# A closing projection: more chunks with seven block products, remainders added by DMA, squares a chunk later

## The chip, the cores and the metric

The kernel runs on one core of one Trainium2 chip. The metric is device time in microseconds (us), from the core's own execution, as a median over runs. The engines have short names in the profile: PE is TensorE (matrix products; PEld is the loading of its stationary operand), DVE is VectorE, ACT is ScalarE, POOL is GpSimd, and SP is SyncE, which here issues most of the loads. A trailing q (SPq, POOLq) means the engine's queue of DMA issues.

## The reference

The program is a two-layer trunk over 256 tokens of width 2048, in float32. The part that matters here is its end: the second layer's feed-forward block, its down projection, the residual and the final norm.

```python
def conv_ffn(xn, w_up, conv_w, conv_b, w_down):
    S = xn.shape[1]
    h = xn @ w_up
    hp = jnp.pad(h, ((0, 0), (CONV_W - 1, 0), (0, 0)))
    h = sum(hp[:, k:k + S] * conv_w[k] for k in range(CONV_W)) + conv_b
    gate, val = jnp.split(h, 2, axis=-1)
    return (jax.nn.silu(gate) * val) @ w_down
...
    h = h + conv_ffn(rmsnorm(h, f_norm[l]), f_w_up[l], f_conv_w[l], f_conv_b[l], f_w_down[l])
...
return rmsnorm(h, final_norm)
```

`w_down` is 5632 x 2048, the activations are 256 x 5632, the result 256 x 2048. Everything before this projection is the same in both kernels.

## The kernel before, in words

**Products in three parts.** Every large product is computed in a rounded 32-bit format (fp32r). Each operand is split into a rounded part (`whi`, ScalarE, line 110 or 88) and a remainder (`wlo`, VectorE: the value less the rounded part, line 111 or 89). A product of two split operands is then three matrix products: rounded x rounded, rounded x remainder, remainder x rounded.

**The stream.** `Stream` takes a list of items, one for each weight chunk of 512 KB (128 partitions x 1024 values). At step i of its `run` it issues, in this order, the load of item i + 6 on SP's queue (line 78), the split of item i + 3, the products of item i, and one step of each side task that is pending (`advance`). Engines work in order on what they are given and wait on semaphores. Raw chunks lie in four buffers used in turn (a ring), the split parts `whi` and `wlo` in four each. So a load waits until the raw chunk four chunks back has been split, and a split waits until the products of the item four back are done.

**The closing projection** has 88 chunks. Its output is worked on by token (128 tokens in each of two blocks, `tb`), 512 columns at a time for blocks 0 to 2 and 256 at a time for the last 512 columns (`short_block` and `last_block`). A plain chunk covers 256 rows of `w_down` and 512 columns: 24 products 256 columns wide.

**Seven products in place of eight.** A chunk can be seen as a 2 x 2 grid of blocks on both sides: two blocks of rows, two halves of the columns, two blocks of tokens. Eight block products can be had from seven, if sums of blocks are formed first (a scheme of Strassen's kind). Such a chunk takes two items: `seven` forms the weight sums (`weight_sums`, lines 490 to 493) and splits three of the raw blocks (line 88 and 89, 768 wide) for the first item, and splits the four sums (1024 wide) for the second. The first item has 9 products 256 columns wide, the second 12, together 21. The sums of the activations are formed once, in pairs of chunks, by `sums_of_blocks` into `X1`, which is free by then. What several chunks add to common partial results is collected in a second PSUM tile `m` and folded into the residual stream `h` by `sums_into_residual` (lines 564 to 580). Before, 1 chunk of block 0 and 8 each of blocks 1 and 2 go this way.

**Behind each block,** the side task `final(blk)` adds the block to `h` (line 435), squares it for the norm with a sum along the row (line 436, ScalarE), and multiplies by the final norm's gains (line 449). `output` (lines 625 to 648) ends the program: the last columns' sum of squares, the root, the scaling, the stores. In `last_block` the products of the first 128 tokens are finished first, and those of the last four chunks for the other 128 are held back, so that the first output overlaps them (`HELD` = 4).

The order of chunks is made by `order_of`, which spreads the seven-product chunks evenly among the plain ones.

Of the kernel before, what the change touches and what calls it, by code (L numbers as in the profile page):

```python
# [17 lines left out]
P = 128  # L18
D = 2048
# [15 lines left out]
SUMMED = (4, 5, 8, 9, 12, 13, 16, 17)  # L35
# [9 lines left out]
class Stream:  # L45
# [38 lines left out]
    def two_parts(self, src, at):  # L84

        n = src.shape[1]
        hi, lo = self.room(at)
        self.nc.scalar.activation(hi[:, :n], src, AF.Copy)
        self.nc.vector.tensor_tensor(lo[:, :n], src, hi[:, :n].bitcast(F32), op=OP.subtract)  # L89
        return hi, lo  # L90
# [70 lines left out]
def order_of(blk):  # L161


    some = SUMMED[:1] if blk == 0 else SUMMED
    plain, seven = [c for c in range(KF // 2) if c not in some], list(some)
    head = 19 if blk == 0 else 2
    out = [(c, False) for c in plain[:head]]
    plain = plain[head:]
    n, m = len(plain), len(seven)
    for i, c in enumerate(plain):  # L170
        while len(seven) * n > (n - i - 1) * m and seven:
            out.append((seven.pop(0), True))
        out.append((c, False))
    return out


def build(ctx, tc, d, out):
# [259 lines left out]

    def final(blk):
        def done(ps):
            while state["summed"] < min(blk + 1, 3):  # L440
                yield
            ss = ph.keep("ss", [P, 2, 5])
            n = ps.shape[2]
            cols = slice(blk * 512, blk * 512 + n)
            for tb in range(2):
                add_block(tb, cols, ps[:, tb, :], ss[:, tb, blk:blk + 1])
                yield
                hh = by_token()[:, tb, cols]
                nc.vector.tensor_tensor(hh, hh, ph.keep("gains", [P, D])[:, cols], op=OP.mult)
                yield  # L450
            if blk == 3:
                v, nv = ph.keep("v", [P, 2]), ph.keep("nv", [P, 2])
                nc.vector.tensor_reduce(v, ss[:, :, :4], axis=AX.X, op=OP.add)
                nc.vector.tensor_scalar(v, v, 1.0 / D, EPS, op0=OP.mult, op1=OP.add)
                nc.vector.tensor_scalar(nv, v, -0.5, None, op0=OP.mult)
# [3 lines left out]
    def block_sums():  # L459

        return X1.rearrange("p (q r) w -> p q (r w)", r=2).rearrange("p q (f l t) -> p q f l t", f=4, l=2)

    def sums_of_blocks(q, pair):

        H = ffn_h()
        x, f = (room().rearrange("p (q i t) -> p q i t", q=2, i=4) for _ in range(2))
        hi, lo = (block_sums()[:, q:q + 2, :, i, :] for i in range(2))
# [747 lines left out]
```

## Time and profile before

| | |
|---|---|
| median of 3 runs | 2180.82 us (2178.99 to 2181.57) |
| profiled execution | 2178.91 us, its span from first to last instruction 2177.0 us |
| granted TensorE clock | 0.999 |
| TensorE busy | 2165.4 us, 99% of the span, 18689 products |
| VectorE busy | 1535.1 us, 71% |
| ScalarE busy | 1163.4 us, 53% |
| GpSimd busy | 27.4 us, 1% |
| bytes moved by DMA | 447.32 MB, 205 GB/s on average |

A row of a group reads: line, engine, operation, output and inputs by the program's names, shapes, count, then the busy time of the group and the mean time of one in ns, then the time for which the engine stood idle before such an instruction and what ended it. A row of a timeline gives start and duration in us, and in brackets the idle time ahead of it. A row of stretches gives the window, then for each engine its busy time and its count of instructions, then the granted clock, the share of the DMA engines and GB/s. A row of a wait gives who waited for whom, the total in us, how many times and the longest. A row of DMA issues ends with the median time from issue to landing. TensorE's instructions overlap in its pipeline, so the durations listed for single products exceed the distance between them.

### The profile page before, as it was taken

To read this page: it belongs to the slowest core of one execution; us is meant where nothing else is said; L and a number is where in the kernel's file an instruction comes from. 1 tells how busy PE (TensorE), PEld (TensorE's weight loads), DVE (VectorE), ACT (ScalarE), POOL (GpSimd) and SP (SyncE) were. 2 spreads that over 40 slices of the span, in tenths; PEclk is the share of its full clock that TensorE was granted. 3 is DMA by queue.
4 is the path that set the end of the run, shared out by engine and by line. 5 is a ranking of instruction groups with operands and counts; after the bars stand their busy time and mean duration, and the time that the engine had idled before them with its cause. 6 is when DMAs were issued, how large, how long until landed. Compare 5 with 4: busy or idle time off the path is not lost.

```text
span 2177.0 us, 45111 instructions
## 1 busy us (share of the span) xinstructions
PE 2165.4 (99%) x18689; PEld 2148.9 (99%) x18689; DVE 1535.1 (71%) x2188; ACT 1163.4 (53%) x1560; POOL 27.4 (1%) x46
## 2 busy tenths in 40 slices
PE   9999999999999999999999999999999999999998
PEld 9999999999999999999999999999999999999998
DVE  6696687777777745556787676678777777778874
ACT  6665555555555544444554665546555555554553
POOL 0000000000000000000001200000000000000000
PEclk9999999999999999999999999999999999999999
DMA  8686565565666566666778776567756565655574
GB/s 312 191 245 200 192 198 194 187 201 188 200 192 195 195 193 195 194 194 184 246 238 263 235 220 199 184 223 220 246 194 194 194 194 187 201 191 177 196 215 153
DMA packets 153230, 447.32 MB, mean 205 GB/s; under 512 B 25584, under 2 KB 44800, under 8 KB 152640
## 3 DMA queue, kind: packets, MB, share of 16 engines
q1 hardware_dynamic: 151488, 440.48, 63.1%
q0 software_dynamic: 1072, 3.41, 0.6%
q8 instruction: 146, 2.39, 0.5%
q10 hardware_dynamic: 464, 0.55, 0.1%
q14 instruction: 60, 0.49, 0.1%
HBM read 430.72 MB, written 13.65 MB: 204 GB/s over the span
## 4 chain that ended last, share of the span: by engine, by line
PE 99%; DVE 1%; DMA 0%; ACT 0%; SPq 0%; issue 0%; DVEq 0%; ACTq 0%
PE ps L212 97%; PE mp L1072 0%; DMA mlp_vt<-a_in_v 0%; DVE wlo L111 0%; ACT whi L110 0%; PE ps L1067 0%; PE ps L1066 0%; PE ps L1065 0%; PE mp L1071 0%; DVE wlo L89 0%; DVE h L435 0%; SPq L78 0%; ACT sq L436 0%; SPq L652 0%; DVE h L647 0%
## 5 line engine op out<-in xcount | busy, mean ns | idle before, releaser
L111 DVE TENSOR_TENSOR wlo<-raw,whi 128x1024 fp32r<-128x1024 f32 x761 | 923.7, 1219 | 390.6 <-ACT whi L110 386.9
L110 ACT ACTIVATE whi<-raw 128x1024 fp32r<-128x1024 f32 x761 | 800.8, 1058 | 674.3 <-PE ps L212 599.2
L212 PE MATMUL ps<-X,whi 128*128 128x256 f32 (+1 forms) x6476 | 824.0, 279 | 0.0
L212 PEld LDWEIGHTS ps<-X,whi 128*128 128x128 f32 x6476 | 776.2, 188 | 6.5
L212 PE MATMUL ps<-X,wlo 128*128 128x256 f32 x3328 | 445.3, 276 | 0.0
L212 PEld LDWEIGHTS ps<-X,wlo 128*128 128x128 f32 x3328 | 409.9, 188 | 1.6
L212 PE MATMUL ps<-whi,ffn_H 128*128 128x256 f32 (+1 forms) x1232 | 201.5, 277 | 0.5 <-ACT whi L110 0.4
L212 PE MATMUL ps<-whi,X 128*128 128x256 f32 (+1 forms) x1136 | 183.1, 279 | 0.4 <-ACT whi L110 0.4
L212 PEld LDWEIGHTS ps<-whi,ffn_H 128*128 128x128 f32 x1232 | 172.9, 188 | 1.3 <-ACT whi L110 0.9
L212 PE MATMUL ps<-ffn_H,whi 128*128 128x256 f32 x1408 | 173.9, 276 | 0.0
L822 DVE SCALAR_TENSOR_TENSOR ffn_room<-ffn_room,col 128x255 f32<-128x255 f32 x352 | 161.8, 481 | 6.4
L212 PEld LDWEIGHTS ps<-ffn_H,whi 128*128 128x128 f32 x1408 | 166.1, 188 | 0.0
L212 PE MATMUL ps<-whi,att_X 128*128 128x256 f32 (+2 forms) x970 | 164.3, 285 | 0.0
L212 PEld LDWEIGHTS ps<-whi,X 128*128 128x128 f32 x1136 | 155.0, 188 | 2.0 <-ACT whi L110 0.6
L212 PE MATMUL ps<-wlo,ffn_H 128*128 128x256 f32 (+1 forms) x615 | 139.2, 277 | 1.5 <-DVE wlo L111 1.5
L212 PEld LDWEIGHTS ps<-whi,att_X 128*128 128x128 f32 x970 | 135.3, 188 | 3.5
L388 DVE TENSOR_TENSOR ffn_room<-ps,rB 128x512 f32<-128x512 f32 x76 | 52.6, 692 | 116.1 <-PE ps L212 116.1
L818 ACT ACTIVATE ffn_room<-ffn_room,col 128x256 f32<-128x256 f32 x176 | 96.3, 595 | 50.0 <-DVE ffn_room L388 50.0
L212 PE MATMUL ps<-wlo,X 128*128 128x256 f32 (+1 forms) x566 | 116.7, 279 | 0.0
L212 PE MATMUL ps<-wlo,att_X 128*128 128x256 f32 (+2 forms) x476 | 105.4, 286 | 0.0
L212 PEld LDWEIGHTS ps<-wlo,ffn_H 128*128 128x128 f32 x615 | 101.1, 188 | 2.0 <-DVE wlo L111 1.9
L212 PE MATMUL ps<-ffn_H,wlo 128*128 128x256 f32 x704 | 94.1, 276 | 0.0
(196 smaller groups left out, 1518.0 us busy)
## 6 DMA issues: line engine op xcount, KB each, us to landing
raw<-up SPq DMA_DIRECT2D x352, 512.0 KB, 4.1
raw<-down SPq DMA_DIRECT2D x154, 512.0 KB, 4.2
raw<-a_in_u SPq DMA_DIRECT2D x32, 512.0 KB, 4.2
raw<-a_out SPq DMA_DIRECT2D x32, 512.0 KB, 3.9
raw<-b_q SPq DMA_DIRECT2D x32, 512.0 KB, 4.5
raw<-kvf_v SPq DMA_DIRECT2D x32, 512.0 KB, 4.9
raw<-b_g SPq DMA_DIRECT2D x32, 512.0 KB, 4.4
raw<-b_out SPq DMA_DIRECT2D x32, 512.0 KB, 4.0
```

What stands on the lines that cost most here:

```text
L110: self.nc.scalar.activation(h, raw, AF.Copy)
L111: self.nc.vector.tensor_tensor(l, raw, h.bitcast(F32), op=OP.subtract)
L212: nc.tensor.matmul(o, a, b, start=start, stop=stop, skip_group_check=True)
L388: nc.vector.tensor_tensor(a, src, rB[:, None, :].to_broadcast([P, 2, T]), op=OP.mult)
L818: nc.scalar.activation(c[:, m, :], a[:, m, :], AF.Identity, scale=w[2], bias=column(C_CONVB + l * 2 * KF + f))
L822: nc.vector.scalar_tensor_tensor(c[:, m, n:], a[:, m, :T - n], w[k], c[:, m, n:], op0=OP.mult, op1=OP.add)
```

## The change

The projection becomes four blocks of 512 columns, all through `seven_block`. Which chunk is of which kind is written out by hand in `ORDERS`: P is plain, S has seven products, D is plain with an added remainder. Block 0 has 22 P; blocks 1 and 2 have P P and five times S D S P; block 3 has ten S, five D and seven P. So S goes from 17 to 30. The chunks with sums are now always the first ten, and the sums of their activations take less room: one of four sums is written over a block of the activations `H` that no later product reads as it was.

In a D chunk VectorE has nothing to do. `added_parts` lets ScalarE write the negated rounded value into `lo`, lets a DMA on GpSimd's queue add the raw chunk to it, with source and destination in SBUF, and lets ScalarE write the rounded value into `hi`. The products with `lo` are put last in such a chunk (`late`): 16 products with `hi`, then 8 with `lo`.

`final` puts a step between the addition and the square, so that the square is issued a chunk after the addition; the last step of `sums_into_residual` comes one chunk earlier. In block 3 the last four plain chunks are held back for the second token block, as `last_block` did; the two column halves of that block are finished one after the other, `closing` squares the first half while the second's products run, and `output` ends as before. The load of ScalarE's table for the square root moves from block 3's end to block 2's.

```diff
-SUMMED = (4, 5, 8, 9, 12, 13, 16, 17)
+PLAIN, SEVEN, ADDED = range(3)
+SUMMED = tuple(range(10))
+ORDERS = ("P" * 22, "PP" + "SDSP" * 5, "PP" + "SDSP" * 5, "PSDSPSDSSDSPSDSSDSPPPP")
...
+    def added_parts(self, src, at):
+
+        hi, lo = self.room(at)
+        self.nc.scalar.activation(lo, src, AF.Copy, scale=-1.0)
+        self.nc.gpsimd.dma_start(lo, src, accum_op=OP.add)
+        self.nc.scalar.activation(hi, src, AF.Copy)
         return hi, lo
...
+    kinds = ["PSD".index(k) for k in ORDERS[blk]]
+    seven = list(SUMMED[:kinds.count(SEVEN)])
+    others = [c for c in range(KF // 2) if c not in seven]
+    return [((seven if k == SEVEN else others).pop(0), k) for k in kinds]
...
     def final(blk):
         def done(ps):
-            while state["summed"] < min(blk + 1, 3):
-                yield
...
+            while state["summed"] < blk:
+                yield
+            ss, gains, _, _ = kept()
+            cols = slice(blk * 512, (blk + 1) * 512)
             for tb in range(2):
-                add_block(tb, cols, ps[:, tb, :], ss[:, tb, blk:blk + 1])
-                yield
                 hh = by_token()[:, tb, cols]
-                nc.vector.tensor_tensor(hh, hh, ph.keep("gains", [P, D])[:, cols], op=OP.mult)
-                yield
...
+                nc.vector.tensor_tensor(hh, hh, ps[:, tb, :], op=OP.add)
+                yield
+                nc.scalar.activation(sq, hh, AF.Square, accum_out=ss[:, tb, blk:blk + 1])
+                yield
+                nc.vector.tensor_tensor(hh, hh, gains[:, cols], op=OP.mult)
+            if blk == 2:
                 nc.scalar.activation(warm, ones, AF.Sqrt)
...
+    def closing(tb, half, ps):
+
+        ss, gains, v, nv = kept()
+        v, nv, r = (a[:, tb:tb + 1] for a in (v, nv, rcol))
+        o = by_token()[:, tb, :]
+        assert state["summed"] == 3
+        if not half:
+            cols = slice(1536, 1536 + T)
+            add_block(tb, cols, ps, ss[:, tb, 3:4])
+            nc.vector.tensor_tensor(o[:, cols], o[:, cols], gains[:, cols], op=OP.mult)
+            nc.vector.tensor_reduce(v, ss[:, tb, :4], axis=AX.X, op=OP.add)
+            nc.vector.tensor_scalar(v, v, 1.0 / D, EPS, op0=OP.mult, op1=OP.add)
+            nc.vector.tensor_scalar(nv, v, -0.5, None, op0=OP.mult)
+        else:
+            output(tb, ps)
...
+        own = sums_kept()[:, q:q + 2]
+        for hi, lo, src in ((own[:, :, :, 0, :], own[:, :, :, 1, :], f[:, :, 1:, :]),
+                            (other[:, :, 0, 1, :], other[:, :, 1, 1, :], f[:, :, 0, :])):
+            nc.scalar.activation(hi, src, AF.Copy)
+            nc.vector.tensor_tensor(lo, src, hi.bitcast(F32), op=OP.subtract)
...
+        def tiles(c, i, hi, lo, tbs, halves, wide=0, late=False):
+            todo = [(j, tb, o) for j in range(2) for tb in tbs for o in ((0, hi), (0, lo), (1, hi))]
+            if late:
+                todo.sort(key=lambda o: o[2][1] is lo)
...
+                if close and i > last - HELD:
+                    held.append((c, i, hi, lo))
+                    tiles(c, i, hi, lo, (0,), (0, 1))
+                else:
+                    tiles(c, i, hi, lo, (0, 1), (0, 1), 0 if close else wide_next(), kind == ADDED)
...
             nc.vector.tensor_tensor(hh[:, :, :T], hh[:, :, :T], m[:, 1:, :T].to_broadcast([P, 2, T]), op=OP.add)
-            yield
             nc.vector.tensor_tensor(hh[:, :, :T], hh[:, :, :T], one[:, 1:, :], op=OP.subtract)
...
-    for blk in range(3):
-        seven_block(blk, d["down1"][22 * blk:22 * blk + 22], order_of(blk), final(blk), sums_into_residual(blk))
-    short_block(d["down1s"][:11], ffn_h, KF, final(3))
-    last_block(d["down1s"][11:], ffn_h, KF)
+    for blk in range(4):
+        seven_block(blk, d["down1"][22 * blk:22 * blk + 22], final(blk), sums_into_residual(blk),
+                    closing if blk == 3 else None)
...
-    arrays["down1"], arrays["down1s"] = tok_chunks(down1[:, :1536]), feat_chunks(down1[:, 1536:])
+    arrays["down1"] = tok_chunks(down1)
```

More of the change, by code (lines that the diff above doesn't have):

```diff
@@ L556, in seven @@
             s.chunk(None, mult_sums, TOK_AT, split=lambda _: s.two_parts(held["t"], TOK_AT))
-        for i, (c, s7) in enumerate(order):
-            if s7:
-                seven(c, i, not any(f for _, f in order[:i]))
+        for i, (c, kind) in enumerate(order):
+            if kind == SEVEN:
+                seven(c, i)
             else:
-                plain(c, i)
+                plain(c, i, kind)
     def sums_into_residual(blk):
```

143 lines of the change are left out of this document (63 added, 80 removed).

## The prediction

> **What bounds the kernel now.** I read the page first, its busy times and its chain of waits.
>
> ```profile
> PE 2165.4 (99%) x18689; PEld 2148.9 (99%) x18689; DVE 1535.1 (71%) x2188; ACT 1163.4 (53%) x1560; POOL 27.4 (1%) x46
> PE 99%; DVE 1%; DMA 0%; ACT 0%; SPq 0%; issue 0%; DVEq 0%; ACTq 0%
> ```
>
> TensorE is busy for 99% of the span and is 99% of the chain. A change gains only by giving it fewer products or by taking away an instant in which it waits. The chain in order of time gives the price of a product, the stretches of the closing projection what is lost there now.
>
> ```profile
> 2139.98 29.37 PE ps L212 x259
> ...
> 2169.37 0.43 DVE h L435
> ...
> 1934.00:1990.00 56.00, 56.00 (x492) 55.87 (x491) 47.07 (x56) 27.91 (x30) 0.00 (x0) 1.00 0.62 201
> 1990.00:2052.00 62.00, 61.12 (x537) 60.73 (x537) 52.65 (x69) 32.35 (x37) 0.00 (x0) 1.00 0.62 202
> 2052.00:2112.00 60.00, 58.85 (x517) 58.45 (x516) 49.89 (x62) 31.19 (x35) 0.00 (x0) 1.00 0.64 199
> 2112.00:2142.00 30.00, 30.00 (x267) 30.00 (x267) 16.64 (x18) 13.32 (x17) 0.00 (x0) 1.00 0.63 198
> 1030.00:1090.00 60.00, 60.00 (x532) 60.00 (x531) 46.88 (x87) 33.56 (x44) 0.00 (x0) 1.00 0.75 246
> ```
>
> 29.37 us over 259 products are 0.1134 us for one 256 columns wide. So a plain chunk (24 products) takes 2.72 us, a seven-product chunk (21) 2.38 us: its first item (9) 1.02, its second (12) 1.36. In the two stretches from 1990 and from 2052 TensorE stands still for 0.88 + 1.15 = 2.03 us; elsewhere in the projection it does not. The waits and the timelines of ScalarE and VectorE tell why:
>
> ```profile
> PE ps L212 <- DVE wlo L111: 1.5, 2, 0.8
> PE ps L212 <- ACT whi L110: 0.4, 1, 0.4
> ...
> 2002.72 0.68 DVE L435 TENSOR_TENSOR h<-h,ps 128x512 f32<-128x512 f32 x1
> ...
> 2003.43 0.63 ACT L436 ACTIVATE sq<-h 128x512 f32<-128x512 f32 x1 [2.15 <-DVE h L435]
> 2003.97 0.19 ACT L436 ACTIVATION_READ_ACCUMULATOR sq<-h 128x1 f32 x1
> 2004.06 1.99 ACT L110 ACTIVATE whi<-raw 128x1024 fp32r<-128x1024 f32 x2
> ```
>
> ScalarE works in order. The square of line 436 is issued straight behind VectorE's addition, so ScalarE idles 2.15 us before it, and the roundings queued behind it (L110), which the next plain chunk needs, come late; the remainder follows them. That happens once in block 1 and once in block 2.
>
> **The change, part by part.** (1) Fewer products. Chunks with seven products go from 1 + 8 + 8 to 10 + 10 + 10, 13 more, each with 3 products fewer: 39 x 0.1134 = **-4.42 us**, all on the chain.
>
> (2) The square comes one chunk later, when the addition is long done, and block 3's squares are ordered the same way. That removes the wait in which both stalls begin: **-2.03 us**; kept, it costs them again (a rival below). What stands ahead of the square instead is the rounding of the next chunks, which ScalarE does at once.
>
> (3) More splitting on VectorE and ScalarE:
>
> ```profile
> L111 DVE TENSOR_TENSOR wlo<-raw,whi 128x1024 fp32r<-128x1024 f32 x153 | 186.1, 1222 | 69.3 <-ACT whi L110 69.1
> L110 ACT ACTIVATE whi<-raw 128x1024 fp32r<-128x1024 f32 x153 | 161.8, 1061 | 132.4 <-PE ps L212 124.7 <-issue 2.3 <-ACT X L477 2.2
> L89 DVE TENSOR_TENSOR wlo<-ffn_room,whi 128x1024 fp32r<-128x1024 f32 x17 | 20.8, 1225 | 5.8 <-ACT whi L88 5.8
> L88 ACT ACTIVATE whi<-ffn_room 128x1024 fp32r<-128x1024 f32 x17 | 18.1, 1064 | 26.0 <-DVE ffn_room L493 20.0 <-PE ps L212 5.7
> L89 DVE TENSOR_TENSOR wlo<-raw,whi 128x768 fp32r<-128x768 f32 x17 | 16.2, 952 | 0.0
> L88 ACT ACTIVATE whi<-raw 128x768 fp32r<-128x768 f32 x17 | 14.4, 844 | 11.1 <-PE ps L212 9.9 <-ACT X L477 0.7 <-ACT whi L110 0.5
> L490 DVE TENSOR_TENSOR ffn_room<-raw 128x512 f32<-128x512 f32 x17 | 11.7, 685 | 0.0
> L493 DVE TENSOR_TENSOR ffn_room<-raw,ffn_room 128x256 f32<-128x256 f32 x17 | 7.2, 426 | 0.6
> L212 PE MATMUL ps<-whi,ffn_H 128*128 128x256 f32 x1226 | 199.6, 276 | 0.5 <-ACT whi L110 0.4
> ...
> 1933.17 3.48 DVE L111 TENSOR_TENSOR wlo<-raw,whi 128x1024 fp32r<-128x1024 f32 x3
> ```
>
> A seven-product chunk (S) costs VectorE 0.685 + 2 x 0.426 + 0.952 + 1.225 = 3.7 us, a plain one (P) 1.2, one with an added remainder (D) nothing; ScalarE 1.9, 1.06 and 2.12. The repeated group S D S P gives VectorE 8.6 us and ScalarE 6.9 in TensorE's 90 products, 10.2 us: hidden. Block 3 is the densest: from its first P to its last S ten S and three P are 40.6 us, and block 2's sums and additions (three of 0.68, two of 0.42, four of 0.69) bring 5.6: 46.2 on VectorE against 10 x 2.38 + 8 x 2.72 = 45.6 on TensorE. But independent instructions there overlap by about 0.1 us (three of 1.222 take 3.48), some 3 us if half of the fifty do, and remainders may trail by a chunk. I take 0, and up to 2 us if that cover is gone. The fifth pair of block sums (by these sizes 1.22 + 0.69 + 0.95 + three of 0.43, some 4 us of VectorE) lies in block 0, now all plain at 1.2 us in each 2.72. The last chain, from 2169.37, keeps its instructions; the first half's square and product fall under the second half's 24 products (2.72 us). 0.
>
> (4) The 15 additions by DMA decide the rest. ScalarE writes the negated rounding (1.06 us), POOL issues a 512 KB SBUF-to-SBUF addition, and its landing lets TensorE start the remainder products. POOL queues nothing else in this stage, so only TensorE and, for the raw buffer, SP's queue of loads wait for it. Call the time from issue to landing X. Three limits follow, with 0.1 us, an allowance of mine, for each handing from engine to queue.
>
> First, a D's room comes free when the item four places earlier ends. In S D S P that leaves 24 + 9 + 12 products, and 16 rounded products of D's own before the first remainder: 61 x 0.1134 = 6.92. A product is listed for 276 ns but the next starts 113 later, so the end is seen 0.2 late; less that, 1.06 and 0.2 for handings: **X up to 5.45**. Second, where two S stand ahead (twice in block 3) it is 49 products: **X up to 4.1**. Third, raw has four buffers in a ring, and in S D S P the load for the next D goes into the buffer which this D's DMA still reads. So load + 1.06 + X + 0.3 must fit into 10.2 us. The loads:
>
> ```profile
> raw<-down SPq DMA_DIRECT2D x154, 512.0 KB, 4.2
> raw<-b_q SPq DMA_DIRECT2D x32, 512.0 KB, 4.5
> raw<-kvf_v SPq DMA_DIRECT2D x32, 512.0 KB, 4.9
> att_cB<-cd POOLq DMA_DIRECT2D x16, 128.0 KB, 4.8
> out<-h SPq DMA_DIRECT2D x6, 256.0 KB, 3.0
> out<-h ACTq DMA_DIRECT2D x2, 256.0 KB, 2.7
> ffn_gains<-final POOLq DMA_DIRECT2D x1, 1024.0 KB, 6.4
> ...
> L1014 POOL DMA_DIRECT2D att_cB<-cd x16: 539/557/557, 1155.2 to 1259.7; - x16
> L78 SPq DMA_DIRECT2D raw<-down x154: 327/328/657, 736.9 to 2093.6; - x154
> ```
>
> Four loads and one addition in 10.2 us are about 255 GB/s; b_q's loads, in the stretch from 1030 at 246 GB/s, took 4.5. So **X up to 4.35**, and what goes beyond it is paid at each D that follows another in a ring, once the first one's lead (5.45 - X) is used.
>
> No row shows an accumulating DMA. Below: 2.7 us, 256 KB out of SBUF. Above: 6.4, 1 MB on POOL's queue, as if the addition moved its bytes twice. Between, POOL's 128 KB at 4.8 and 1 MB at 6.4 give 5.5 for 512 KB; the load of the same 512 KB in the same 4 KB rows in this stage, 4.2, plus POOL's longer issue (0.557 against 0.328), gives 4.4. I take **4.4**: it matches in size, rows and traffic, while the 128 KB rows are small reads from DRAM in a busier stage, and an SBUF source was not slower (2.7 to 3.0). Cost at 4.4: two dense D's x 0.3 and one ring step of 0.05, **+0.65 us**; the ring steps in blocks 1 and 2 are covered by the lead of 1.05.
>
> [...]
>
> Sum: -4.42 - 2.03 + 0.65 = -5.8 us. The profiled execution took 2178.91 us (span 2177.0 and 1.9 around it), 1.9 under the runs' median, so it would come to 2173.1, and the median of 2180.82 to **2175.0 us**. With X at 4.1 or less it is -6.45: 2174.4.
>
> **The rivals.** *The addition lands late* (slower). With a = X - 4.35, d = X - 4.1 and lead = 5.45 - X, blocks 1 and 2 each pay 4a - lead, block 3 pays (a - lead) + 2d + a, each not below zero (from 5.45 on every first D pays X - 5.45 too). At X = 5.5 that is 2 x 4.65 + 1.2 + 2.8 + 1.15 = 14.45 us, net +8.0: **2188.8**. At 6.4 it is 28, net +21.5: 2202. It outweighs the gain from X = 4.97 on, and the time is more than 0.2% slower (4.36 us, about what a measurement here can tell from no change) from 5.26 on. For it speak POOL's own two rows, which give 5.5, and that an addition must read its destination; against it the 4.4 above.
>
> *It lands a little late* and eats the gain: X from 4.63 to 5.26, net -4.3 to +4.3; at 4.95 the cost is about 6.2: **2180.6**. Loads of 4.9, as kvf_v's, move it here as well (the ring's limit becomes 3.95, the cost at 4.4 about 2.6, net -3.9).
>
> *The later square doesn't remove the stalls*, because VectorE's weight sums, not the wait, hold up the roundings at the start of a block: the 2.03 stays, net -3.8: **2177.0**. For it: ScalarE also waited 20.0 us in all on L493; against it: each of the two stalls follows directly on a square.
>
> **How the numbers follow.** Landing in time 0.40 (2173.5 to 2176.5 by itself), a little late 0.20, stalls that stay 0.05, late 0.35. So faster 0.40, same 0.25, slower 0.35. The range goes from 2173.5 to 2197, which is X at about 6.0; the rest of the late case, some 0.13, and 0.05 below are left out.
>
> **What would show it.** The products of line 212 fall by 39. POOL shows 15 DMA issues in the last 240 us; their time to landing is X, 4.4 by my forecast. TensorE's waits on those DMAs should be under 1 us in all, and only in block 3; a wait in each group of blocks 1 and 2 that grows along the block means that the ring binds. TensorE should no longer wait for a rounding that is queued behind a square. I am wrong if landings exceed 5 us, or if TensorE waits for VectorE's remainders in block 3.

## The result, and the profile after

The change made the kernel slower: 2191.55 us median (2188.83 to 2195.17, 6 runs) against 2179.01 us (2178.61 to 2181.57, 6 runs) of the kernel before, a ratio of 1.0056, 95% interval 1.0043 to 1.0069. The profiled execution took 2188.83 us (span 2187.0), 9.9 more than the one before. Since it is the changed kernel's shortest run, the medians differ by more, 12.5 us. Of the forecasts it is the rival in which the addition lands late that has the right sign.

First TensorE's row of the busy times, then what TensorE's weight loads waited for from 1930 us to the end (us in all, times, longest):

```profile
PE 2167.2 (99%) x18650; PEld 2148.5 (98%) x18650; DVE 1555.1 (71%) x2238; ACT 1189.6 (54%) x1594; POOL 39.3 (2%) x61
```

```profile
PEld ps L215 <- DMA wlo<-raw: 8.1, 8, 2.3
PEld ps L215 <- DVE h L438: 2.7, 1, 2.7
PEld ps L215 <- DVE wlo L91: 1.4, 3, 0.5
PEld ps L215 <- ACT whi L99: 1.2, 2, 0.8
PEld ps L215 <- DVE wlo L121: 0.3, 1, 0.3
PEld ps L215 <- issue: 0.2, 1, 0.2
```

The 39 products are gone (18689 to 18650). The same waits of the weight loads were 2.8 us in the kernel before (1.9 for remainders, 0.9 for roundings); now they are 13.9 us, 8.1 of them for additions. The end of the chain shows a second loss:

```profile
2171.77 0.34 DVE h L438
...
2172.15 4.51 PE ps L215 x24
2176.66 2.73 PE mp L215 x24
```

In the closing TensorE waits 2.7 us for VectorE's line 438, and the 24 products behind that wait take 4.51 us, where the next 24 take 2.73. The same stretch in slices of 1 us (busy time and instructions of PE, PEld, DVE, ACT and POOL, then the granted clock, the share of the DMA engines and GB/s) says why:

```profile
2172.00:2173.00 1.00, 0.85 (x4) 0.85 (x5) 0.68 (x4) 0.80 (x3) 0.00 (x0) 0.50 0.00 0
2173.00:2174.00 1.00, 1.00 (x6) 1.00 (x6) 0.89 (x5) 0.30 (x1) 0.00 (x0) 0.50 0.00 0
2174.00:2175.00 1.00, 1.00 (x7) 1.00 (x6) 1.00 (x4) 0.43 (x1) 0.00 (x0) 0.50 0.00 0
2175.00:2176.00 1.00, 1.00 (x9) 1.00 (x8) 0.11 (x1) 0.00 (x0) 0.00 (x0) 0.82 0.82 303
2176.00:2178.00 2.00, 2.00 (x20) 2.00 (x20) 0.73 (x2) 0.51 (x2) 0.00 (x0) 1.00 0.98 365
```

The granted clock is at 0.50 from 2172.0 until about 2175.4, where the products follow at 0.213 us in place of 0.1134, and at 1.00 in the row from 2176; the 24 products take 4.51 - 2.73 = 1.8 us longer.

The three stretches of the stage that the prediction read, in the same columns:

```profile
1990.00:2052.00 62.00, 60.69 (x525) 59.89 (x524) 46.10 (x59) 37.70 (x42) 4.33 (x5) 1.00 0.75 228
2052.00:2112.00 60.00, 58.26 (x503) 57.39 (x502) 51.30 (x70) 38.94 (x44) 4.54 (x6) 1.00 0.80 239
2112.00:2142.00 30.00, 26.10 (x215) 24.94 (x214) 26.45 (x39) 18.98 (x24) 2.31 (x3) 1.00 0.77 208
```

TensorE now stands still for 1.3, 1.7 and 3.9 us in them (0.9, 1.2 and 0 before), and block 3 is the worst.

The sum closes nearly, if the projection is taken by itself. In this execution it begins 1.0 us earlier than in the one before (its first product starts at 1931.39 against 1932.36), and its last product ends 10.0 us later (2179.39 against 2169.37), so it takes 11.0 us longer. The products gave -4.42, as forecast. Against them the waits of the weight loads grew by 11.1: 8.1 (additions), 2.7 (closing) and 3.1 (roundings, remainders and issue), less the 2.8 of before. The slow products of the closing cost 1.8. Another 1.8 us lies between the waits, in the pace of the products. The first two rows are the same 14 us in the changed kernel and in the kernel before, the third is of the changed kernel's chain:

```profile
2142.00:2156.00 14.00, 14.00 (x121) 14.00 (x120) 10.63 (x15) 9.36 (x10) 1.71 (x2) 1.00 0.77 244
2142.00:2156.00 14.00, 14.00 (x126) 14.00 (x125) 8.17 (x12) 7.43 (x10) 0.00 (x0) 1.00 0.46 155
...
2141.95 2.12 PE ps L215 x18
```

TensorE counts as busy throughout and its clock as whole, but 18 products take 2.12 us, 0.1178 each, where the kernel before has 0.1134. By the starts of all products of the projection, 400 of them follow at the longer distance, which is the 1.8 us. The terms make 10.3 us; the last 0.7 are delays of under 0.2 us between single products.

The additions themselves, with their issue on GpSimd (ns, least, median and most) and their time from issue to landing:

```profile
L98 POOL DMA_DIRECT2D wlo<-raw x15: 847/856/895, 1995.4 to 2154.9; - x15
...
DMA to landing us min/median/max: 4.8/5.2/5.9
```

X is 5.2 us, not 4.4. In block 1 the chain runs through the ring of raw buffers, which the prediction had as its third limit:

```profile
2006.38 5.45 DMA wlo<-raw
...
2011.88 3.51 DMA raw<-down
...
2015.46 1.62 issue
...
2017.09 5.91 DMA wlo<-raw
```

An addition ends, the load that waited for its buffer starts, the next addition follows. From 2006.38 to 2017.09 that is 10.7 us a group, and 11.0 in the next two, where the products of a group take 10.2.

### The profile page after: what moved, and what is told of

Its sections match the earlier page's. It is cut to its first block, busy times and chain, and to the rows that moved or that the text cites. A ratio compares the mean times of both kernels' runs of the same rounds, so it can differ in the third digit from the quotient of the medians.

```text
span 2187.0 us, 45178 instructions
## 1 busy us (share of the span) xinstructions
PE 2167.2 (99%) x18650; PEld 2148.5 (98%) x18650; DVE 1555.1 (71%) x2238; ACT 1189.6 (54%) x1594; POOL 39.3 (2%) x61
## 4 chain that ended last, share of the span: by engine, by line
PE 94%; DMA 3%; issue 1%; DVE 1%; ACT 0%; POOL 0%; POOLq 0%; DVEq 0%; ACTq 0%; SPq 0%
PE ps L215 93%; DMA wlo<-raw 2%; DMA raw<-down 1%; PE mp L215 0%; PE mp L1102 0%; PE mp L710 0%; ACT whi L90 0%; PE ps L1096 0%; PE ps L1097 0%; PE ps L1095 0%; PE mp L1101 0%; DVE wlo L91 0%; DVE wlo L121 0%; ACT wlo L97 0%; ACT L459 0%
## 5 line engine op out<-in xcount | busy, mean ns | idle before, releaser
L121 DVE TENSOR_TENSOR wlo<-raw,whi 128x1024 fp32r<-128x1024 f32 x733 | 890.9, 1220 | 366.3 <-ACT whi L120 358.5
L120 ACT ACTIVATE whi<-raw 128x1024 fp32r<-128x1024 f32 x733 | 771.6, 1058 | 656.5 <-PE ps L215 578.9
L215 PE MATMUL ps<-whi,X 128*128 128x256 f32 (+1 forms) x1180 | 197.9, 279 | 0.0
L215 PE MATMUL ps<-whi,ffn_H 128*128 128x256 f32 (+1 forms) x1094 | 182.8, 279 | 3.4 <-DVE h L438 2.5
L215 PEld LDWEIGHTS ps<-whi,X 128*128 128x128 f32 x1180 | 164.9, 188 | 1.3
L215 PEld LDWEIGHTS ps<-whi,ffn_H 128*128 128x128 f32 x1094 | 154.4, 189 | 4.5 <-DVE h L438 2.7
L215 PE MATMUL ps<-wlo,X 128*128 128x256 f32 (+1 forms) x588 | 123.2, 280 | 0.5 <-DVE wlo L91 0.5
L215 PE MATMUL ps<-wlo,ffn_H 128*128 128x256 f32 (+1 forms) x546 | 113.1, 281 | 6.9 <-DMA wlo<-raw 6.3
L215 PEld LDWEIGHTS ps<-wlo,ffn_H 128*128 128x128 f32 x546 | 85.3, 189 | 9.1 <-DMA wlo<-raw 8.1
```

The lines of the kernel that those rows point to most:

```text
L120: self.nc.scalar.activation(h, raw, AF.Copy)
L121: self.nc.vector.tensor_tensor(l, raw, h.bitcast(F32), op=OP.subtract)
L215: nc.tensor.matmul(o, a, b, start=start, stop=stop, skip_group_check=True)
```

## The experiments

All times are medians beside the kernel before in the same comparison; the ratio and its interval compare all runs of both kernels and need not be the quotient of the two medians. The comparisons ran on different chips, so small differences between two experiments go by their intervals. "Waits for additions" are those of TensorE's weight loads in the profiled execution.

### Seven-product chunks without additions

Each D becomes a plain chunk; all else stays.

```
-ORDERS = ("P" * 22, "PP" + "SDSP" * 5, "PP" + "SDSP" * 5, "PSDSPSDSSDSPSDSSDSPPPP")
+ORDERS = ("P" * 22, "PP" + "SPSP" * 5, "PP" + "SPSP" * 5, "PSPSPSPSSPSPSPSSPSPPPP")
```

> The changed kernel with every D chunk made plain, so no addition by DMA; the 30 seven-product chunks and all else stay. Theory: the additions are the largest loss (TensorE waits 8.1 us for them), but VectorE then has 9.8 us of remainders and sums in each group's 10.2 and over 50 in block 3's 45.6, so at least half of the loss comes back as waits for VectorE: between 2187 and 2195, and TensorE's waits go to lines 91 and 121 in place of the DMA. Rival one: VectorE's overlap carries it, the 8.1 us go altogether: 2183.5. Rival two: without the additions VectorE is so far over that it is slower than the changed kernel by more than 5 us: above 2197; then the D chunks pay for themselves.

Measured: 2184.04 us against 2179.48, ratio 1.0011 [1.0002, 1.0020]. So some 7.5 of the 12.5 us by the medians come with the additions, net of the work that they spare VectorE, and without them there is no gain either. The time is near that of the first rival, but VectorE's overlap does not carry the load: this kernel's own waits for VectorE and ScalarE are 8.9 us, 2.7 of them in the closing. One of them shows the halved clock in the middle of the stage. The first row is TensorE's timeline, the others slices of 1 us:

```profile
2111.40 0.36 PE L215 MATMUL ps<-whi,ffn_H 128*128 128x256 f32 x1 [1.80 <-DVE h L625]
```

```profile
2112.00:2113.00 1.00, 1.00 (x9) 1.00 (x9) 0.96 (x2) 0.00 (x0) 0.00 (x0) 0.78 0.76 283
2114.00:2115.00 1.00, 1.00 (x6) 1.00 (x6) 0.97 (x2) 0.67 (x1) 0.00 (x0) 0.50 0.00 0
2116.00:2117.00 1.00, 1.00 (x11) 1.00 (x11) 0.82 (x1) 1.00 (x3) 0.00 (x0) 1.00 0.92 340
```

A wait of 1.80 us, and from about 2112.6, 1.2 us after it, the clock is at half until 2116. The wait is for line 625, the folding of block 2's sums, on an engine that is busy for 3.38 of the 3.41 us from 2109.15 on. It is VectorE's crowding at the head of block 3, which the prediction had costed at 0.

### The DMAs copy instead of adding

The addition is left out here: the DMA overwrites the negated rounding with the raw chunk.

```
-        self.nc.gpsimd.dma_start(lo, src, accum_op=OP.add)
+        self.nc.gpsimd.dma_start(lo, src)
```

> The changed kernel with the 15 DMAs as plain copies of the same 512 KB: the addition is left out, so those chunks' remainders are the raw chunks themselves. Asks what the addition itself costs. Theory: the time from issue to landing is that of the path and of the bytes moved once, and the addition adds its second read: 4.3 us or less in place of 5.2, issue 0.56 in place of 0.86, TensorE's waits for these DMAs from 8 to under 3 us. Rival: an addition costs no more than a copy, the 5.2 us are POOL's queue and the traffic: 5.0 to 5.3, waits as before, 2189.

```profile
L98 POOL DMA_DIRECT2D wlo<-raw x15: 528/531/540, 1996.1 to 2148.5; - x15
...
DMA to landing us min/median/max: 2.9/4.0/5.0
```

```profile
PEld ps L215 <- DVE h L438: 2.5, 1, 2.5
PEld ps L215 <- DMA wlo<-raw: 1.0, 3, 0.4
```

Measured: 2180.11 us (one run). A copy lands in 4.0 us, and GpSimd's issue takes 0.53 us instead of 0.86. With it the waits for the DMAs nearly vanish (1.0 of 8.1 us). So the 4.4 us of the prediction was a copy's price, if anything; the addition is 1.2 us dearer.

### Addition and copy with nothing beside them

Blocks 1 to 3 load only their first chunk and use it for all others (the other loads are left out, and with them the right weights); all engine instructions and all 15 DMAs stay. The second kernel copies as above, so it leaves the addition out too.

```
+        if place == "same":
+            self.raw[i] = self.same
+            return
...
-            s.chunk(src[c], mult, TOK_AT, split=...)
+            s.chunk(src[c], mult, TOK_AT, place="same" if blk and i else None, split=...)
...
```

> The changed kernel without the weight loads of blocks 1 to 3 but each block's first: every other chunk of a block takes its weights from that first one's place (so its sums are not the reference's). Every instruction of the engines and all 15 additions stay. What is measured is an addition with nothing beside it on the 16 DMA engines. Theory (an addition is dear because it shares the engines with loads that come in bursts, and reads twice): issue to landing falls from 5.2 us to about 4, 3.5 to 4.4, and TensorE's waits for additions from 8 to 9.5 us to under 2. Rival (5.2 us is the addition's own time, whatever runs beside it): 4.8 to 5.2 us, and the waits of blocks 1 and 3 stay above 4 us, since the own budget is as short as before.

> The same with the DMA copying in place of adding (the addition is left out as well). Theory: a copy with nothing beside it lands in about 3 us (the shortest in the changed kernel with copies took 2.9 with loads beside some of them), about 1 us before an addition alone; issue on GpSimd 0.53 us. Rival: both land in the same time alone, the difference of 1.2 us with loads beside them being only their share of the engines.

The landing rows, of the additions first, then of the copies:

```profile
DMA to landing us min/median/max: 4.5/4.5/5.7
```

```profile
DMA to landing us min/median/max: 2.9/2.9/5.1
```

An addition alone takes 4.5 us, already more than the 4.4 forecast under traffic; a copy takes 2.9. Each theory got one part: it is not a matter of traffic alone (4.5 is above the 4.4 that the theory allowed at most), and the difference between addition and copy, 1.6 us alone, is the addition's own. Beside loads it is 5.2, so 0.7 us come from traffic. The waits for additions fell from 8.1 to 4.8 us, not to under 2. Of these, 4.3 lie in block 3. The longest, 2.0, is behind the addition whose negation comes late (see the table load below); where two S stand ahead (limit 4.1) 4.5 is late as well. The kernel with additions took 2185.32 us in its one run, the one with copies 2179.16.

### Is it the ring of raw buffers?

Two twins with fewer additions: blocks 1 and 2 go PP, four times S D S P, PPPP; block 3 has none. In the second the raw chunks of D lie in two places of their own behind the block sums (8 KB of each partition that are free with four pairs of sums), so no load waits for an addition. Those eight loads are then issued by GpSimd, so this twin differs in the queue too.

```
-SUMMED = tuple(range(10))
+SUMMED = tuple(range(8))
-ORDERS = ("P" * 22, "PP" + "SDSP" * 5, "PP" + "SDSP" * 5, "PSDSPSDSSDSPSDSSDSPPPP")
+ORDERS = ("P" * 22, "PP" + "SDSP" * 4 + "PPPP", "PP" + "SDSP" * 4 + "PPPP", "PPSPSPPSPSPPSPSPPSPPPP")
```

and in the second twin alone

```
-        self.nc.sync.dma_start(raw, src)
+        (self.nc.sync if raw.dtype == F32 else self.nc.gpsimd).dma_start(raw, src)
...
+            at = KD * 2 * T - CHUNK * (1 + state["added"] % 2)
+            apart = X1.rearrange("p a w -> p (a w)")[:, at:at + CHUNK] if kind == ADDED else None
-            s.chunk(src[c], mult, TOK_AT, split=...)
+            s.chunk(src[c], mult, TOK_AT, place=apart, split=...)
```

> The changed kernel with eight seven-product chunks in blocks 1 and 2 (four groups S D S P, then four plain chunks), seven in block 3 spread out and no addition there: 8 additions and 18 products fewer than before. It is the twin of the next kernel. Ring theory (the next addition's raw chunk can only be loaded when the addition before it has let go of the same buffer, so a step takes load 4.4 + negation 1.06 + addition 5.2 + handing 0.3 = 11.0 us against 10.2 of products): the additions of block 1 are issued 10.8 to 11.1 us apart, and TensorE waits 2 to 4 us for additions in blocks 1 and 2 together. Rival (each addition is late by its own budget, 5.2 + 0.6 of handing against 5.45 + 0.3): the same steps, which only the next kernel tells apart. Time about 2179.5 - 2.0 - 3.4 + 3 for the additions + 4.5 for the closing = 2181.6.

> The twin of the kernel before it with one difference: the raw chunks that are copied by DMA lie alternately in two places of their own (free room of 4 KB each behind the kept block sums), so that no load waits for an addition. Those places hold fp32r, so these 8 loads are issued by GpSimd. Ring theory: steps of 10.2 to 10.4 us in block 1, waits for additions under 1 us in blocks 1 and 2 together, 2 to 3 us faster than its twin. Rival (own budget): the steps and the waits stay as in the twin, the time within 0.8 us of it.

TensorE's waits for additions, in the twin with the ring and in the one without:

```profile
PEld ps L215 <- DMA wlo<-raw: 3.7, 6, 0.9
```

```profile
PEld ps L215 <- DMA wlo<-X: 2.6, 5, 0.9
```

Measured: 2182.90 and 2182.78 us, ratios 1.0013 [1.0004, 1.0022] and 1.0012 [1.0002, 1.0021]. In block 1 the issues lie 11.0, 11.1 and 10.5 us apart in the one, 11.2, 10.7 and 10.5 in the other. So taking the ring away in this way gains 1.1 us of waits and no time that can be told apart, and the rival's steps and time came true. The additions land at 5.6 us (5.5 with the ring), above their own budget of 5.45. But the edit also puts a load beside each addition: GpSimd issues one 0.56 us behind it (at 2007.96 and 2008.52, for one). So the ring is not the only limit; what it would give with the loads out of the way is not shown. Products that follow at 0.1178 us cost these executions another 3.5 and 3.9 us, as much as the waits for additions or more.

### More time for each addition

The same chunks in an order that puts two plain chunks ahead of each addition.

```
-ORDERS = ("P" * 22, "PP" + "SDSP" * 4 + "PPPP", "PP" + "SDSP" * 4 + "PPPP", ...)
+ORDERS = ("P" * 22, "P" + "SPPDS" * 4 + "P", "P" + "SPPDS" * 4 + "P", ...)
```

> The kernel of eight_ring with the same chunks in another order: blocks 1 and 2 go P, four groups S P P D S, P instead of P P, four groups S D S P, four P. An addition now has two plain chunks and a seven-product chunk between the moment its room comes free and its first remainder: 24 + 24 + 12 + 16 = 76 products, 8.6 us, in place of 61, 6.9 us, so the time from issue to landing may be 8.6 - 0.2 - 1.06 - 0.5 = 6.9 us where it was 5.2 with the handings seen so far. Own-budget theory: the additions take the same 5.2 to 5.9 us to land, and TensorE's waits for them (3.7 us in eight_ring) fall under 0.5; the time falls by some 3 us against eight_ring, to a ratio of about 1.000 with the kernel before. Ring theory: a plain chunk's load still waits for the addition, and waits for additions or for roundings behind it stay above 2 us. Rival (the transfers slow each other or TensorE whatever the order): the waits go and the time stays.

```profile
DMA to landing us min/median/max: 6.4/8.0/9.3
```

```profile
2007.18 4.54 DMA raw<-down
...
2011.82 1.07 ACT wlo L97
...
2013.18 9.28 DMA wlo<-raw
...
2022.50 5.22 PE ps L215 x29
```

My theory failed: 2191.75 us, ratio 1.0055 [1.0041, 1.0069], 9 us above the twin, with 8.0 us of waits for additions. The 6.9 us of budget were met by landings of 8.0. The chain shows a load that had been held up, the negation behind it, and an addition of 9.28 us. From 2013 to 2022 the DMA engines move 176 to 257 GB/s, most of it other loads, and after the wait of 2.07 us the granted clock was at 0.50 from about 2023.1 to 2026.5 (29 products in 5.22 us; at 0.1134 us each they take 3.3).

> The kernel of eight_early (additions with a budget of 6.9 us from issue to landing) with the copied chunks' raw weights in two places of their own, loaded by GpSimd's queue, as in eight_apart, so that no load is held up behind an addition and none comes in a burst behind it. Theory (the 6.4 to 9.3 us of eight_early were loads released together with the next addition, by the ring): issue to landing 5.2 to 6.0 us, waits of TensorE for additions under 0.5 us (8.0 in eight_early), time some 9 us below eight_early, a ratio of 0.999 to 1.001 with the kernel before. Rival (three loads run beside the addition in this order, ring or not): landings of 7 us or more, waits of several us, the time within 4 us of eight_early.

The same order with the places apart, its landings and its waits:

```profile
DMA to landing us min/median/max: 6.5/7.5/8.0
```

```profile
PEld ps L215 <- DMA wlo<-X: 3.5, 5, 1.2
```

Measured: 2184.63 us, ratio 1.0016 [1.0006, 1.0026]. Taking the ring away gives 7 us back in this order: 4.5 us less waiting, and no halved clock before the last product, where the order with the ring had three (the mean granted clock of the span is 0.999 against 0.997). That is more than the 4 us that the rival allowed. But the landings stay at 7.5 us, as the rival said: in this order loads run beside the additions with the ring, and without it GpSimd issues one 0.56 us behind each. X is no constant of the operation; it runs from 4.5 us alone over 5.2 to 7.5 and 8.0 with the loads beside it.

### The closing

The second token tile's first half gets a PSUM tile of its own, so that its products need not wait for VectorE's reading of the first tile.

```
-                    box["end"] = misc_ps()
-            if close and tb and half:
-                return box["end"][:, :T]
+                    box["end"] = [misc_ps(), misc_ps()]
+            if close and tb:
+                return box["end"][half][:, :T]
```

> The changed kernel, but the second token block's first column half of block 3 is summed in a PSUM tile of its own instead of the second bank of the tile that also holds the first token block. Theory: in the changed kernel the held products wait 2.73 us because that shared tile is still being read by VectorE's additions (line 438), and the 24 products behind the gap take 4.51 us in place of 2.72 because the granted clock falls to 0.66 and 0.77 after it. Then the wait and the low clock both go: 4.5 us less than the changed kernel, 2187 by the medians, about +0.37% against the kernel before. Rival: the wait is on the additions themselves (VectorE is late with block 3's sums), whatever the tile: then the wait stays and the time is 2191.5, as the changed kernel. Second rival: only the wait goes and the slow products are slow for another reason: 2.7 us less, 2189.

The first two rows are VectorE's timeline, the last TensorE's wait for additions:

```profile
2173.84 0.42 DVE L438 TENSOR_TENSOR h<-h,ps 128x256 f32<-128x256 f32 x1 [0.62 <-PE ps L215]
...
2178.96 0.41 DVE L438 TENSOR_TENSOR h<-h,mp 128x256 f32<-128x256 f32 x1
```

```profile
PEld ps L215 <- DMA wlo<-raw: 9.5, 8, 2.2
```

Measured: 2190.13 us, ratio 1.0040 [1.0026, 1.0053], 1.4 us less than the changed kernel by the medians, which the two intervals don't tell apart. The wait for line 438 and the halved clock are gone, as expected (the granted clock is 1.00 from 2120 to 2180). But the two tiles' closings lie on VectorE one behind the other, 5.1 us each, the last starts some 1.3 us later than TensorE's end would allow; this execution waited 1.4 us more for additions, and 1.5 us more went into products that follow at 0.1178 us. So the 4.5 us are gone as expected, and these three terms, 4.2 us, nearly make up for them.

### The table load in block 3

In the changed kernel the longest idle time before a remainder product is in block 3. TensorE's timeline there, and ScalarE's:

```profile
2132.07 0.62 PE L215 MATMUL ps<-wlo,ffn_H 128*128 128x256 f32 x3 [2.06 <-DMA wlo<-raw]
```

```profile
2124.47 1.28 ACT L459 ACT_TABLE_LOAD   x1
...
2125.87 1.04 ACT L97 ACTIVATE wlo<-raw 128x1024 fp32r<-128x1024 f32 x1
```

The load of the square-root table, 1.28 us, stands ahead of that addition's negation (L97). It was moved to the first held chunk:

```
-            if blk == 2:
-                nc.scalar.activation(warm, ones, AF.Sqrt)
...
+                    if not held:
+                        nc.scalar.activation(warm, ones, AF.Sqrt)
```

> The changed kernel with one line moved: the square-root table is loaded at the first held chunk of block 3, not behind block 2's last square. Theory (the table load of 1.28 us stands ahead of the second addition's negation in block 3 and makes it late): the longest wait of TensorE for an addition there falls from 2.06 us to under 1, that addition is issued 1.2 to 1.5 us after the first negation could start, and the span is about 1.5 us shorter than 2187.0. Rival (VectorE's crowding holds the square ahead of the negation, so the load only fills time in which ScalarE would wait anyway): the wait stays at 1.7 us or more and the span within 0.5 us.

Measured: 2187.70 us (one run, span 2186.0 against 2187.0). The idle time before that product fell from 2.06 to 1.37 us, between the theory's 1 and the rival's 1.7. The waits for additions are 9.1 us in all, and in this execution the closing's 24 products took 3.01 us in place of 4.51, more than the whole difference of 1.0 us between the spans. No gain is shown.

### The changed kernel once more

> The changed kernel once more, for one other execution. Theory (the same waits in every execution, the spread of its times being where they fall): waits for additions between 7 and 11 us in all, the closing's wait of 2.3 to 2.7 us; the granted clock after that wait is 0.5 or 1.00 by chance, since the same wait left it at 1.00 in two executions of its relatives and halved it in others. Rival: the halving belongs to this kernel and is there again, with 24 products in 4.5 us.

Measured: 2192.22 us, 9.5 us of waits for additions, 2.5 in the closing. The closing's 24 products took 3.01 us, so the halving there is not this kernel's own, as the theory had it. Instead the granted clock was at 0.50 from 2134.3 to 2137.7 and from 2165.0 to 2168.4, each time behind idle time of 2.0 to 2.1 us before an addition's products, some 1.7 us lost each. So the two executions differ in which waits a halved clock followed, once in the one and twice in the other; whether that makes the spread of the changed kernel's runs was not shown.

### What is left of the gain

The later square, with the last step of the block sums a chunk sooner, put into the kernel before:

```
-                add_block(tb, cols, ps[:, tb, :], ss[:, tb, blk:blk + 1])
-                yield
+                nc.vector.tensor_tensor(hh, hh, ps[:, tb, :], op=OP.add)
+                yield
+                nc.scalar.activation(sq[:, :n], hh, AF.Square, accum_out=ss[:, tb, blk:blk + 1])
...
             nc.vector.tensor_tensor(hh[:, :, :T], hh[:, :, :T], m[:, 1:, :T].to_broadcast([P, 2, T]), op=OP.add)
-            yield
```

> The kernel before with the square a chunk after the addition and the sums' last step a chunk sooner, nothing else. The prediction's step: TensorE's two stalls of 0.88 and 1.15 us go, 2.03 us less, -0.09%: 2177. Rival: VectorE's crowding at the start of a block, not the order of the square, makes them: less than 0.7 us, and a wait of TensorE for a rounding or remainder stays in both blocks.

Measured: 2176.09 us against 2179.48, ratio 0.9979 [0.9970, 0.9988]. In the stretches in which the kernel before lost 2.03 us TensorE now never stands still:

```profile
1990.00:2052.00 62.00, 62.00 (x549) 62.00 (x549) 54.51 (x70) 33.92 (x39) 0.00 (x0) 1.00 0.63 204
2052.00:2112.00 60.00, 60.00 (x531) 60.00 (x531) 51.76 (x66) 32.37 (x36) 0.00 (x0) 1.00 0.67 209
```

From its first product to its last the projection takes 233.9 us (1936.35 to 2170.21), where the kernel before takes 237.0, 3.1 less. Which of the two edits does it was not tried. The profiled execution itself took 2179.79 us, one of the two long ones of eleven: a load of `b_q`, ahead of the projection, has 1% of its chain, TensorE is listed busy for 2168.1 us where the kernel before has 2165.4, and it entered the projection 4.0 us late.

And the changed kernel without additions, its 23 seven-product chunks spread out, with the tile of the closing and the late table load:

```
+SUMMED = tuple(range(8))
+ORDERS = ("P" * 22, "PP" + "SPSPP" * 4, "PP" + "SPSPP" * 4, "PPSPSPPSPSPPSPSPPSPPPP")
```

> The changed kernel without any addition by DMA, with the seven-product chunks spread out (8, 8 and 7 of them, never two in a row, a plain chunk or two between), the closing's second token tile in a PSUM tile of its own, and the square-root table loaded at the first held chunk instead of behind block 2's squares. 18 products fewer than before (39 in the changed kernel), so -2.04 us; the later square gave -3.4 by itself. Theory (the products are worth their 0.1134 us each wherever VectorE keeps up, and what the changed kernel lost was lost to additions, to crowding and to the closing's shared tile): 2179.5 - 2.0 - 3.4 + up to 1.3 for VectorE's closing chain = 2174 to 2175.5, TensorE's waits for remainders under 0.5 us in all, granted clock 1.00 up to TensorE's last product. Rival (VectorE can't bear more seven-product chunks at all): waits for VectorE's remainders of 1 us or more come back, and the time is that of the later square alone or above it, 2176 to 2179.

Measured: 2175.00 us (2174.03 to 2175.61, 10 runs) against 2180.56, ratio 0.9975 [0.9966, 0.9985]. It beats both kernels; with 18671 products TensorE has no wait left in the stage. What the 18 products add to the later square the runs do not tell apart, since the intervals overlap, but the profiled executions do: the projection takes 231.8 us (1932.49 to 2164.30), 2.0 less than with the later square alone, and 18 x 0.1134 is 2.04. Some 1.3 us of that is lost again, as VectorE's closing chain starts that much late here as well.

> The kernel of spaced (closing's second token tile in a PSUM tile of its own, the table load late, block 3 spread out) with the order of eight_early in blocks 1 and 2: eight additions by DMA, none of them due before 6.9 us after its issue; 18 products fewer than before, as in spaced. Theory (an addition in time costs nothing, and buys nothing where VectorE keeps up without it): ratio with the kernel before within 0.0007 of spaced's 0.9975, no wait of TensorE for an addition of more than 0.3 us. Rival (additions cost TensorE something beyond waits): 1 us or more above spaced.

> The kernel of spaced_early (the closing's second token tile in a PSUM tile of its own, the table load late, block 3 spread out, eight additions due 6.9 us after issue) with the copied chunks' raw weights in places of their own. Theory (an addition that lands in time costs nothing, and buys nothing where VectorE keeps up): waits for additions under 0.5 us, ratio 0.9975 with the kernel before, as in spaced, within 0.0010. Rival: additions cost TensorE something even without waits, and the ratio is 0.999 or more.

The same kernel with eight additions in the order of more time, with the ring 2189.19 us, ratio 1.0042 [1.0029, 1.0056], and with places apart 2184.43 us, ratio 1.0019 [1.0009, 1.0028]. TensorE's waits for additions are 7.2 and 4.7 us. The profiled execution of the latter took 2180.93 us, 5.8 above that of the kernel without additions, which is near its 4.7 + 0.6 us of waits and the 0.5 us that products at 0.1178 us cost it. I expected no cost for an addition in time; none of these orders has one in time, so that was not tested.

## Why the prediction was wrong

**Fewer products (step 1): right.** 39 products are gone, and the count holds for the 18 of the spread kernel too.

**The later square (step 2): right, and undersized.** With the sums' earlier last step it gave 3.4 us by the medians (interval 2.6 to 6.5) and 3.1 in the projection, where 2.03 were forecast. TensorE's weight loads had waited 2.8 us in the kernel before, against the 2.03 of idle products that I summed: a product is listed to its end, 0.28 us, and the next could have started 0.11 after it.

**More splitting (step 3): wrong.** It was set at 0, with up to 2 us if the cover is gone. Roundings and remainders cost 2.9 us of waits, and without any addition 6.2; the closing cost 2.7 more in both. The step "the first half's square and product fall under the second half's 24 products" looked at VectorE's instructions and not at the tile: the second token tile's first products were to be written into the PSUM tile from which VectorE still had to read the first one's second half. They waited 2.7 us, and the halved clock added 1.8. No row of the kernel before shows that wait, since there each token tile had a PSUM tile of its own; the changed code did show it. Nor did the prediction price what a wait costs beyond its length, the halved clock and the slower pace.

**The additions (step 4): the step that failed is "I take 4.4".** It took the landing of a load of the same size, and the runs show that as a copy's price (4.0 beside loads, 2.9 alone). An addition takes 4.5 alone and 5.2 here. The prediction had a reason in its text, that an addition must read its destination, and put it with the rival; that the second read is what makes the difference is not shown apart from the rest of the operation. With X = 5.2 the formula behind the step gives 2 x 3.15 for blocks 1 and 2 and 0.6 + 2.2 + 0.85 for block 3, 9.95 us; 8.1 to 9.5 us of waits were measured. That the totals are so near is partly luck: by block the waits were 2.1, 1.4 and 4.5 us, so blocks 1 and 2 paid less than the formula says and block 3 more, where a negation came late behind the table load. Net the formula would have meant 2182.4 by the profiled execution; step 3's losses, the clock and the slower pace make the rest.

**The limits: half right.** That the ring binds is in the chain. But the prediction took X as fixed while the limits moved, and so did I in the experiments: in the kernels without the ring loads fall beside the additions, X is 5.6 to 7.6, and the next limit is missed.

**The rivals.** The late addition was right in sign and mechanism, but at X = 5.2, which by the prediction's own bounds (4.63 to 5.26) belongs to the addition that is a little late, with a net of +3.5. The time reached the 2188.8 that it gave for X = 5.5 through losses it did not contain. The stalls did not stay.

## What to carry to other kernels

Price an accumulating DMA by itself and not as a copy (here 5.2 us against 4.0 beside loads, 4.5 against 2.9 alone), and give it the worst landing beside a burst of loads rather than the median of a row for something else. Before work is moved to a queue, ask which buffer its transfer holds and which queue stands still behind that buffer (here a load started at 2011.88, behind an addition that ran from 2006.38 to 2011.83). Where two outputs share one PSUM tile, look at whether the writer of the second waits for the reader of the first: here it waited 2.7 us, though they use different halves, and not with a tile of its own. And price a wait of the engine that bounds the kernel at more than its length: in the changed kernel 11.1 us more of waits came with 3.6 us of slower products (1.8 by the clock, 1.8 by the pace).

## What the runs showed of the hardware

The granted clock was at 0.50 behind some of TensorE's waits, for 3.41 us each time: from 2171.95 to 2175.36 in the changed kernel, behind 2.53 us of idle time; from 2112.56 to 2115.97 without additions, behind 1.80; from 2134.31 to 2137.72 and from 2165.03 to 2168.44 in the changed kernel's second execution, behind 2.00 and 2.09. At half the clock that loses 1.7 us each time, half of 3.41 by my estimate, nearly as much as the wait. Other waits as long had no halved clock behind them: 2.06 us in block 3 of the changed kernel's first execution and 2.28 in the closing of its second.

The four changes in the second execution lie 1, 8 and 1 times 3.41 us apart, so I also read the idle time in stretches of that length, counted from the changes. The first three rows are stretches of the changed kernel's first execution, the last of its second:

```profile
2127.58:2130.99 3.41, 2.10 (x16) 1.91 (x16) 2.61 (x4) 2.70 (x4) 0.48 (x1) 1.00 0.81 147
2130.99:2134.40 3.41, 2.33 (x19) 2.33 (x20) 2.79 (x5) 1.20 (x2) 0.00 (x0) 1.00 0.81 246
2168.54:2171.95 3.41, 1.08 (x10) 0.88 (x8) 2.73 (x9) 0.51 (x2) 0.00 (x0) 1.00 0.00 0
...
2130.90:2134.31 3.41, 1.41 (x13) 1.21 (x12) 3.34 (x6) 1.31 (x2) 0.00 (x0) 1.00 1.04 231
```

The 2.06 us lay across two stretches, with 1.3 and 1.1 us idle in them, and the clock stayed at 1.00; the 2.00 us lay in a single one, and the clock was at 0.50 in the next, as it was behind the third row with its 2.3 us. That is what these two executions had; what sets the clock they do not show.

Products 256 columns wide followed one another at 0.1134 us in the kernel before (from 1935.7 on), and at either 0.1134 or 0.1178 in the changed kernel, both at a granted clock of 1.00. From 1935.7 to the closing the distance changed eight times there, each time at a delay between two products (0.35 to 2.33 us from start to start), and other delays left it as it was (0.59 us at 2033.26). What sets it stays open.

GpSimd's issue of an addition took 0.86 us, of a copy 0.53.
